# Sums of squares of the q/k norm: four float32 products a tile in place of twelve bfloat16 ones

## The chip, the cores and the metric

The program runs on one core of a Trainium2 chip. Its time is the device time of one execution in microseconds (us), from the first to the last instruction with what the launch adds around it. The core has five engines that run their own instruction streams: TensorE (PE; its weight loads are listed apart as PEld), VectorE (DVE), ScalarE (ACT), GpSimd (POOL) and SyncE (SP), which only issues transfers here. They wait for one another by semaphores.

## The reference

The reference is two layers of a decoder on 512 positions of width 2048, in float32. Each layer normalizes its input, projects it to queries, keys, values and a gate, attends, multiplies by the gate and projects back:

```python
q = rope(rms_norm(q.reshape(B, T, N_HEADS, HEAD_DIM), q_g), pos)      # 16 heads of 128
k = rope(rms_norm(k.reshape(B, T, N_KV_HEADS, HEAD_DIM), k_g), pos)   # 4 heads of 128
...
def rms_norm(x, g):
    y = xf * lax.rsqrt(jnp.mean(xf * xf, axis=-1, keepdims=True) + EPS)
    return (y * g.astype(jnp.float32)).astype(x.dtype)
```

The first layer picks the 128 best keys of each query by an indexer before it attends; the second attends within blocks of 256, which is the whole causal past for these 512 positions. What matters here is the mean of `xf * xf` over the 128 elements of a head, for each of 16 query heads and 4 key heads of a layer, and each of the 512 positions.

## The kernel before, in words

**Tiles and quarters.** Every projection is worked off in tiles of 128 output columns, held transposed: 128 features on the partitions, 512 positions along the row. A weight is cut into a high and a low part (`whi`, `wlo`), an input into `xh` and `xl`, and a product is made of three: high by high, high by low, low by high (lines 222 to 224). A tile has 16 blocks of the inner dimension, so 48 products of 128x512, and it is issued in four *quarters* of twelve products. The list `units` holds all quarters in their order; the main loop takes one unit a turn, and its index is the time `now` of the program text. In a layer come the values, then for each of four groups a k tile, four q tiles and the gate tiles of these heads, and then 16 output tiles `z_o`.

**What sets the order.** TensorE and SyncE execute in the order in which the text emits instructions, throughout. ScalarE, VectorE and GpSimd do so in the opening (46 units); behind it a scheduler orders their instructions ahead of the run. `later(k, f)` puts a step `f` behind the products of the unit `k` turns on. Two lists of steps concern the norm. A k tile: `s1` (1 turn after its last quarter), `s2` (2), `s2b` (4), `s3` (5), `s4` (6), `s5` (7), `s6` (8). A q tile: `s1` (1), `s2` (2), `s2b` (4), `s3` (5).

**The norm.** The features lie on the partitions, so a sum over a head's 128 features is a sum over partitions, and TensorE makes it: the squares are the stationary operand, a column of ones moves through, and the 128 sums of a block of positions come out as one column. `s1` builds a `Norm`: ScalarE squares the tile (line 306) and rounds the square to bfloat16 (316). `middle`, in `s2`, subtracts the rounded part on VectorE, rounds the rest (320) and subtracts again, so that three bfloat16 parts `b0`, `b1`, `b2` hold the float32 square. `sums`, in `s2b`, multiplies four blocks of positions by three parts, twelve products of one column, into a bank of PSUM (`cs_q` or `cs_k`, line 327). In `s3` VectorE adds the layer's own term (`u_q`, `u_k`) and GpSimd takes the power -1/2 (`sc`, `rk`). For a k tile, `bcast` in `s4` then spreads `rk` over the partitions (`b_k`, line 257), and `s5` and `s6` multiply and cut the key tile. The banks of `cs`, `b_k` and a layer's statistics are one and the same (`psm`, one buffer).

**The statistics of a layer.** `layer_stats` sums the squares of the layer's input over the width. It uses `colsum` (lines 246 to 251), which multiplies the float32 sum of squares `ssum` by a float32 column of ones, in four products (`ss`, line 250), once a layer.

**Paced extra work.** The selection in the first layer is a list `fill` of VectorE steps; the main loop takes from it as long as the paced count of VectorE's work (`dve.until`) lies behind the turn. While the list is not empty, the low parts of weights are cut on GpSimd. When it is empty, the mask opens the first layer's heads (`A.open`), which then attend at distances of 7 or 8 turns.

Of the kernel before, what the change touches and what calls it, by code (L numbers as in the profile page):

```python
# [26 lines left out]
BF = mybir.dt.bfloat16  # L27
AF = mybir.ActivationFunctionType
OP = mybir.AluOpType
# [3 lines left out]
P = 128  # L33
# [3 lines left out]
NQ = T // P  # L37
# [68 lines left out]
def build(tc, a):  # L106
    nc = tc.nc
# [14 lines left out]
    def t512(tag, name, dt=F32, bufs=None, p=None, cols=T):  # L122
        return (p or kp).tile([P, cols], dt, tag=tag, name=name, **({"bufs": bufs} if bufs else {}))
# [4 lines left out]
    def small(tag, name, bufs=2):  # L128
        return kp.tile([P, NQ], F32, tag=tag, name=name, bufs=bufs)

    def ps(tag, name, bufs):
        return pp.tile([P, T], F32, tag=tag, name=name, bufs=bufs)

    pss = lambda name: ps("s", name, 3)
    psm = lambda name: ps("sm", name, 1)
# [10 lines left out]
    def later(k, f, first=False):  # L146
        fs = hooks.setdefault(now[0] + k, [])
        fs.insert(0 if first else len(fs), f)
# [6 lines left out]
    dve, gps = Paced(nc.vector, 1.05e-3), Paced(nc.gpsimd, 2.1e-3)  # L155
# [72 lines left out]
    def add(t, quarters=None):  # L228
        units.extend((t, q) for q in quarters or range(KT // t.kts))
# [7 lines left out]
    ones_bf = cp.tile([P, 1], BF, name="ones_bf")  # L237
# [8 lines left out]
    def colsum(sq, name):  # L246

        t = psm(name)
        for j in range(NQ):
            nc.tensor.matmul(t[:, j:j + 1], lhsT=sq[:, j * P:(j + 1) * P], rhs=ones, start=True, stop=True)  # L250
        return t[:, :NQ]

    def bcast(col, name):

        t = psm(name)
        for j in range(NQ):
            nc.tensor.transpose(t[:, j * P:(j + 1) * P], col[:, j:j + 1].to_broadcast([P, P]), ident)
        return t

    def cut_hi(hi, src):  # L260
        nc.scalar.copy(hi, src)

    def cut_lo(lo, src, hi):
        dve.tensor_tensor(lo, src, hi.bitcast(F32), op=OP.subtract)
# [28 lines left out]
    def rope(z, g, name):  # L293

        t1 = tmp(f"t1_{name}")
        t2 = tmp(f"t2_{name}")
        dve.scalar_tensor_tensor(t1, z, g, cos, op0=OP.mult, op1=OP.mult)
        for o, i in ((0, 64), (64, 0)):
            dve.scalar_tensor_tensor(t2[o:o + 64], z[i:i + 64], g[i:i + 64], sin[i:i + 64],
                                           op0=OP.mult, op1=OP.mult)  # L300
        dve.tensor_tensor(t1, t1, t2, op=OP.add)
        return t1

    def square(z, name):
        sq = t512("sq", f"sq_{name}", bufs=1)
        nc.scalar.activation(sq, z, AF.Square)
        return sq

    class Norm:


        def __init__(self, z, name):
            self.name = name
            self.sq = square(z, name)
            self.b = [t512(f"b{i}", f"b{i}_{name}", BF, bufs=1) for i in range(3)]
            nc.scalar.copy(self.b[0], self.sq)

        def middle(self):
            dve.tensor_tensor(self.sq, self.sq, self.b[0], op=OP.subtract)
            nc.scalar.copy(self.b[1], self.sq)  # L320
            dve.tensor_tensor(self.b[2], self.sq, self.b[1], op=OP.subtract)

        def sums(self):
            t = psm(f"cs_{self.name}")
            for j in range(NQ):
                for i in range(3):
                    nc.tensor.matmul(t[:, j:j + 1], lhsT=self.b[i][:, j * P:(j + 1) * P], rhs=ones_bf,
                                     start=i == 0, stop=i == 2)
            return t[:, :NQ]

    def k_tile(Y, g):
        n = f"k{Y.L}_{g}"
        early = Y.L == 0 and g == 1
        v = SimpleNamespace()

        def s1():
            v.n = Norm(v.z, n)
            v.r = rope(v.z, Y.kg, n)

        def s2():  # L340
            v.n.middle()

        def s2b():
            v.s = v.n.sums()

        def s3():
            u = small("u", f"u_{n}")
            dve.scalar_tensor_tensor(u, v.s, 1.0 / P, Y.ce, op0=OP.mult, op1=OP.add)
            v.rk = small("rk", f"rk_{n}", 1)
            gps.tensor_tensor(v.rk, u, mhalf, op=OP.pow)  # L350

        def s4():
            v.b = bcast(v.rk, f"b_{n}")

        def s5():
            dve.tensor_tensor(v.r, v.r, v.b, op=OP.mult)
            p, th, tl = (bp, "bh15", "bl15") if early else (kp, "kh", "kl")
            kh = t512(th, f"kh_{n}", F32R, p=p)
            kl = t512(tl, f"kl_{n}", F32R, p=p)
            cut_hi(kh, v.r)  # L360
            Y.K[g] = (kh, kl)

        def s6():
            cut_lo(Y.K[g][1], v.r, Y.K[g][0])

        def done(z):
            v.z = z
            for k, f in ((1, s1), (2, s2), (4, s2b), (5, s3), (6, s4), (7, s5), (8, s6)):
                later(k, f)
        add(Tile(n, Y.w[16 + g], Y.X, done))  # L370

    def v_tiles(Y):
# [12 lines left out]
    def q_tile(Y, h):  # L385
        n = f"q{Y.L}_{h}"
        early = Y.L == 0 and h < 8
        v = SimpleNamespace()

        def s1():  # L390
            v.n = Norm(v.z, n)
            v.r = rope(v.z, Y.qg, n)

        def s2b():
            v.s = v.n.sums()

        def s2():
            v.n.middle()
            p, th, tl = (bp, f"bh{9 - h % 4}", f"bl{9 - h % 4}") if early else (kp, "qh", "ql")
            qh = t512(th, f"qh_{n}", F32R, p=p)  # L400
            ql = t512(tl, f"ql_{n}", F32R, p=p)
            cut_hi(qh, v.r)
            cut_lo(ql, v.r, qh)
            Y.q[h] = (qh, ql)

        def s3():
            u = small("u", f"u_{n}")
            dve.tensor_tensor(u, v.s, Y.cq, op=OP.add)
            sc = small("sc", f"sc_{n}", 6)
            gps.tensor_tensor(sc, u, mhalf, op=OP.pow)  # L410
            Y.sc[h] = sc

        def done(z):
            v.z = z
            Y.qslot[h] = now[0]
            for k, f in ((1, s1), (2, s2), (4, s2b), (5, s3)):
                later(k, f)
        add(Tile(n, Y.w[h], Y.X, done))

    def g_tile(Y, h):  # L420
# [132 lines left out]
    def mixer_tiles(Y):  # L553
        if Y.L:
            v_tiles(Y)
        for g in range(HEADS // GROUP):
            k_tile(Y, g)
            for h in range(GROUP * g, GROUP * g + GROUP):
                q_tile(Y, h)
                if h == 1 and not Y.L:  # L560
                    v_tiles(Y)
                if h % GROUP:
                    g_tile(Y, h - 1)
            g_tile(Y, h)
# [29 lines left out]
    def x_square(kt):  # L594
        if kt == 0:
            nc.scalar.activation(ssum, xs[kt], AF.Square)
        else:
            sq = square(xs[kt], f"x{kt}")
            gps.tensor_tensor(ssum, ssum, sq, op=OP.add)
# [159 lines left out]
    def evac0(n, z):  # L759
        def s1():  # L760
            r = res.pop((0, n))
            dve.tensor_tensor(r, z, r, op=OP.add)
            nc.sync.dma_start(h1[n], r)
            take(X1, n, r, gains[:, KT + n:KT + n + 1], 1)
            if n == 0:
                ssum1.append(t512("S", "ssum1", cols=1280)[:, :T])
                nc.scalar.activation(ssum1[0], r, AF.Square)
            else:
                sq = square(r, f"h{n}")
                gps.tensor_tensor(ssum1[0], ssum1[0], sq, op=OP.add)  # L770
        later(1, s1)
        if n == KT - 1:
            later(4, lambda: layer_stats(B, ssum1[0]))
# [25 lines left out]
    for L, start, src in ((0, first_out, a["xT"]), (1, second_out, h1)):  # L799
        for i in range(start, start + 4 * KT):  # L800
            t, q = units[i]
# [121 lines left out]
```

## Time and profile before

| | |
|---|---|
| median of 3 runs | 1481.86 us (1481.7 to 1481.94) |
| the profiled execution's own time | 1481.96 us |
| its span, first to last instruction | 1480.0 us |
| busy: PE / DVE / ACT / POOL | 1472.1 / 912.7 / 698.7 / 149.1 us |

All rows below come from one profiled execution. A row of the timeline begins with the start and the duration in us. Products overlap in TensorE, so durations add up to more than the time they take: the distance between two starts is what a product costs the stream. A group's row gives the busy time, the mean of one in ns, and the idle time of its engine ahead of it with what ended it.

### The profile page before, as it was taken

Reading aid. Unit: us, or ns where it says so; the run is one execution under the profiler, and the core shown is the slowest. Engines: PE = TensorE matmul, PEld = TensorE weight load, DVE = VectorE, ACT = ScalarE, POOL = GpSimd, SP = SyncE. Lnnn points to the kernel's source line nnn. Section 1 sums busy time; section 2 is a strip of 40 time slices with the busy share of each in tenths; the row PEclk is TensorE's granted clock in tenths of the full one; section 3 lists DMA queues with packets and bytes.
Section 4 is the critical chain, followed back from the end, with each engine's and each line's share of the span. In section 5 each row is a group of like instructions: output and inputs, shape, how many; then the busy total and the mean of one; then the engine's idle time right before and its main releaser. Section 6 shows DMA issues by size and latency. Waiting matters only on the chain.

```text
span 1480.0 us, 20172 instructions
## 1 busy us (share of the span) xinstructions
PE 1472.1 (99%) x7318; PEld 1233.0 (83%) x7318; DVE 912.7 (62%) x1845; ACT 698.7 (47%) x1332; POOL 149.1 (10%) x123
## 2 busy tenths in 40 slices
PE   9999999999999999999999999999999999999998
PEld 6998888888888888888888888888888888888887
DVE  6998976767567666643333376676676576643232
ACT  6874244555446445533332345554555455442221
POOL 0442420000010010111110010000000000000000
PEclk9999999999999999999999999999999999999999
DMA  7332324535433524444443224334434433454442
GB/s 252 108 99 74 100 97 145 153 111 144 134 111 118 156 90 139 143 156 150 149 143 114 100 90 152 107 122 144 134 110 123 151 122 107 143 164 150 142 143 92
DMA packets 77283, 191.78 MB, mean 130 GB/s; under 512 B 8704, under 2 KB 25856, under 8 KB 77184
## 3 DMA queue, kind: packets, MB, share of 16 engines
q1 hardware_dynamic: 76896, 189.98, 41.2%
q8 instruction: 57, 0.93, 0.3%
q10 hardware_dynamic: 288, 0.52, 0.1%
q14 instruction: 42, 0.34, 0.1%
HBM read 161.11 MB, written 29.36 MB: 129 GB/s over the span
## 4 chain that ended last, share of the span: by engine, by line
PE 97%; DMA 1%; DVE 1%; ACT 1%; issue 0%; SPq 0%; DVEq 0%; POOL 0%; ACTq 0%; POOLq 0%
PE z_q L222 8%; PE z_g L222 8%; PE z_g L224 8%; PE z_q L224 8%; PE z_g L223 8%; PE z_q L223 8%; PE z_o L223 8%; PE z_o L222 8%; PE z_o L224 8%; PE o L527 4%; PE z_k L222 2%; PE z_v L205 2%; PE z_k L224 2%; PE z_k L223 2%; PE z_v L207 2%; PE z_v L206 2%
## 5 line engine op out<-in xcount | busy, mean ns | idle before, releaser
L222 PE MATMUL z_q<-xh,whi_q 128*128 128x512 f32 x512 | 202.9, 396 | 0.0
L222 PE MATMUL z_g<-xh,whi_g 128*128 128x512 f32 x512 | 202.1, 395 | 0.0
L224 PE MATMUL z_g<-xh,wlo_g 128*128 128x512 f32 x512 | 200.1, 391 | 0.0
L224 PE MATMUL z_q<-xh,wlo_q 128*128 128x512 f32 x512 | 199.9, 390 | 0.0
L223 PE MATMUL z_g<-xl,whi_g 128*128 128x512 f32 x512 | 199.4, 390 | 0.0
L222 PE MATMUL z_o<-bh,whi_o 128*128 128x512 f32 x512 | 199.4, 389 | 0.0
L223 PE MATMUL z_q<-xl,whi_q 128*128 128x512 f32 x512 | 199.4, 389 | 0.0
L224 PE MATMUL z_o<-bh,wlo_o 128*128 128x512 f32 x512 | 199.2, 389 | 0.0
L223 PE MATMUL z_o<-bl,whi_o 128*128 128x512 f32 x512 | 199.2, 389 | 0.0
L89 DVE TENSOR_TENSOR wlo_o<-raw_o,whi_o 128x512 fp32r<-128x512 f32 x128 | 88.8, 693 | 163.4 <-ACT whi_o L192 163.4
L192 ACT CAST whi_o<-raw_o 128x512 fp32r<-128x512 f32 x128 | 79.7, 623 | 229.4 <-PE z_o L223 216.8
L192 ACT CAST whi_g<-raw_g 128x512 fp32r<-128x512 f32 x128 | 79.3, 620 | 166.3 <-PE z_q L223 120.9
L89 DVE TENSOR_TENSOR wlo_g<-raw_g,whi_g 128x512 fp32r<-128x512 f32 x123 | 84.5, 687 | 107.6 <-ACT whi_g L192 107.3
L192 ACT CAST whi_q<-raw_q 128x512 fp32r<-128x512 f32 x128 | 79.1, 618 | 103.9 <-PE z_q L223 43.4
L224 PEld LDWEIGHTS z_q<-xh,wlo_q 128*128 128x128 f32 x512 | 96.1, 188 | 20.9
L224 PEld LDWEIGHTS z_g<-xh,wlo_g 128*128 128x128 f32 x512 | 96.1, 188 | 20.8
L222 PEld LDWEIGHTS z_o<-bh,whi_o 128*128 128x128 f32 x512 | 96.1, 188 | 20.0
L224 PEld LDWEIGHTS z_o<-bh,wlo_o 128*128 128x128 f32 x512 | 96.1, 188 | 19.9
L223 PEld LDWEIGHTS z_o<-bl,whi_o 128*128 128x128 f32 x512 | 96.1, 188 | 19.8
L223 PEld LDWEIGHTS z_q<-xl,whi_q 128*128 128x128 f32 x512 | 96.2, 188 | 18.9
L223 PEld LDWEIGHTS z_g<-xl,whi_g 128*128 128x128 f32 x512 | 96.2, 188 | 18.6
L222 PEld LDWEIGHTS z_q<-xh,whi_q 128*128 128x128 f32 x512 | 96.1, 188 | 18.6
(164 smaller groups left out, 2687.0 us busy)
## 6 DMA issues: line engine op xcount, KB each, us to landing
d<-u SPq DMA_DIRECT2D x64, 320.0 KB, 3.8
pt<-d SPq DMA_DIRECT2D x128, 160.0 KB, 3.6
raw_q<-w_a SPq DMA_DIRECT2D x32, 512.0 KB, 4.1
raw_g<-w_a SPq DMA_DIRECT2D x32, 512.0 KB, 3.9
raw_q<-w_b SPq DMA_DIRECT2D x32, 512.0 KB, 4.4
raw_g<-w_b SPq DMA_DIRECT2D x32, 512.0 KB, 4.3
raw_o<-w_ao SPq DMA_DIRECT2D x26, 512.0 KB, 3.6
raw_o<-w_bo SPq DMA_DIRECT2D x26, 512.0 KB, 3.6
```

The costliest lines, as they stand in the source:

```text
L89: return f(out, *args, **kw)
L192: nc.scalar.copy(hi, r)
L205: nc.tensor.matmul(z, lhsT=xh, rhs=hi, start=first, stop=False)
L206: nc.tensor.matmul(z, lhsT=xh, rhs=lo, start=False, stop=False)
L207: nc.tensor.matmul(z, lhsT=xl, rhs=hi, start=False, stop=last)
L222: nc.tensor.matmul(o, lhsT=hi[:, k], rhs=xh, start=kt == 0, stop=False)
L223: nc.tensor.matmul(o, lhsT=hi[:, k], rhs=xl, start=False, stop=False)
L224: nc.tensor.matmul(o, lhsT=lo[:, k], rhs=xh, start=False, stop=kt == KT - 1)
L527: nc.tensor.matmul(o[:, q], lhsT=Y.V[kt][l][:, f], rhs=r[:, t], start=m == 0 and c == 0, stop=m == 4 and c == 2)
```

## The change

The Norm keeps the float32 squares and gives them to `colsum`. The parts, their roundings and subtractions go, and `middle` with them. The squares have two buffers instead of one. With one step less in between, the sums and what follows them stand one turn earlier: 3, 4, 5, 6, 7 for a k tile and 3, 4 for a q tile.

```diff
     def square(z, name):
-        sq = t512("sq", f"sq_{name}", bufs=1)
+        sq = t512("sq", f"sq_{name}", bufs=2)
...
             self.sq = square(z, name)
-            self.b = [t512(f"b{i}", f"b{i}_{name}", BF, bufs=1) for i in range(3)]
-            nc.scalar.copy(self.b[0], self.sq)
-
-        def middle(self):
-            dve.tensor_tensor(self.sq, self.sq, self.b[0], op=OP.subtract)
-            nc.scalar.copy(self.b[1], self.sq)
-            dve.tensor_tensor(self.b[2], self.sq, self.b[1], op=OP.subtract)
 
         def sums(self):
-            t = psm(f"cs_{self.name}")
-            for j in range(NQ):
-                for i in range(3):
-                    nc.tensor.matmul(t[:, j:j + 1], lhsT=self.b[i][:, j * P:(j + 1) * P], rhs=ones_bf,
-                                     start=i == 0, stop=i == 2)
-            return t[:, :NQ]
+            return colsum(self.sq, f"cs_{self.name}")
...
-        def s2():
-            v.n.middle()
-
...
-            for k, f in ((1, s1), (2, s2), (4, s2b), (5, s3), (6, s4), (7, s5), (8, s6)):
+            for k, f in ((1, s1), (3, s2b), (4, s3), (5, s4), (6, s5), (7, s6)):
...
         def s2():
-            v.n.middle()
...
-            for k, f in ((1, s1), (2, s2), (4, s2b), (5, s3)):
+            for k, f in ((1, s1), (2, s2), (3, s2b), (4, s3)):
```

In TensorE's order, these rows stand at the sums of the second layer's first k tile before. `z_q_0` is the next q tile; the first three products of the block, each with its weight load, are shown, and the block goes on to its twelfth, behind which the q tile `z_q_1` begins.

```order
L223 MATMUL z_q_0_8048<-xl_15_7677,whi_q_0_3_8073 128x512
L224 MATMUL z_q_0_8048<-xh_15_7676,wlo_q_0_3_8074 128x512
L327 LDWEIGHTS b_k_0_8063
L327 MATMUL cs_k_0_8128<-ones_bf,b_k_0_8063 128x1
L327 LDWEIGHTS b_k_0_8064
L327 MATMUL cs_k_0_8128<-ones_bf,b_k_0_8064 128x1
L327 LDWEIGHTS b_k_0_8065
L327 MATMUL cs_k_0_8128<-ones_bf,b_k_0_8065 128x1
```

And these stand there now, in the same engine, around the same tile.

```order
L223 MATMUL z_q_0_7748<-xl_11_7054,whi_q_0_2_7744 128x512
L224 MATMUL z_q_0_7748<-xh_11_7053,wlo_q_0_2_7745 128x512
L250 MATMUL cs_k_0_7803<-ones,sq_k_0_7761 128x1 x4
L222 MATMUL z_q_0_7748<-xh_12_7133,whi_q_0_3_7769 128x512
L223 MATMUL z_q_0_7748<-xl_12_7134,whi_q_0_3_7769 128x512
```

The sums have moved from behind the last quarter of `z_q_0` to behind its third quarter, and four products of the float32 square (`x4`) take the place of twelve. Neither the products of the projections nor their order have changed there.

On GpSimd, these are the rows where the first layer's first k tile gets its scales, before: `rk_k_0` is the power of that tile, `rc` that of the layer's statistics, `acc` the scores of the indexer, and `wlo` a low part of a weight.

```order
L89 TENSOR_TENSOR rc_1369<-ms_1367,mhalf 128x4
L89 AFFINE_SELECT acc_119<-acc_119 128x128
L89 AFFINE_SELECT acc_118<-acc_118 128x128
L89 AFFINE_SELECT acc_117<-acc_117 128x128
L89 TENSOR_TENSOR rk_k_0_1565<-u_k_0_1563,mhalf 128x4
L89 TENSOR_TENSOR wlo_q_1_3_1580<-raw_q_1_2_1340,whi_q_1_3_1579 128x512
```

And now:

```order
L89 TENSOR_TENSOR rc_1369<-ms_1367,mhalf 128x4
L89 TENSOR_TENSOR rk_k_0_1504<-u_k_0_1502,mhalf 128x4
L89 AFFINE_SELECT acc_119<-acc_119 128x128
L89 AFFINE_SELECT acc_118<-acc_118 128x128
L89 AFFINE_SELECT acc_117<-acc_117 128x128
L89 TENSOR_TENSOR wlo_q_1_3_1566<-raw_q_1_2_1340,whi_q_1_3_1565 128x512
```

The power for the k tile has moved ahead of the three selects on the scores. The selection's list is emptied one turn earlier, and the first four heads of the first layer attend one turn earlier than before; the other 28 heads stand at the turns where they stood.

## Rows read from the trace of the kernel before

**Rows 1.** Page, part 1: busy us, share of the span, instructions of each engine.

```profile
PE 1472.1 (99%) x7318; PEld 1233.0 (83%) x7318; DVE 912.7 (62%) x1845; ACT 698.7 (47%) x1332; POOL 149.1 (10%) x123
```

**Rows 2.** Page, part 2: TensorE's granted clock in 40 slices, in tenths.

```profile
PEclk9999999999999999999999999999999999999999
```

**Rows 3.** Page, part 4: the chain that ended last, by engine.

```profile
PE 97%; DMA 1%; DVE 1%; ACT 1%; issue 0%; SPq 0%; DVEq 0%; POOL 0%; ACTq 0%; POOLq 0%
```

**Rows 4.** Windows: start:end, length, busy us (count) of PE, PEld, DVE, ACT, POOL, PEclk, DMA.

```profile
37.00:140.00 103.00, 101.27 (x549) 92.54 (x548) 94.31 (x139) 73.32 (x149) 38.71 (x30) 1.00 0.31 95
222.00:610.00 388.00, 388.00 (x2018) 325.54 (x2017) 265.19 (x575) 205.44 (x408) 23.68 (x17) 1.00 0.44 130
800.00:806.00 6.00, 6.00 (x32) 5.08 (x31) 1.71 (x5) 1.17 (x2) 1.02 (x1) 1.00 0.29 87
```

**Rows 5.** Waits of PE: who waited for whom, us in total, times, longest.

```profile
PE is L676 <- DVE Q L89: 1.3, 2, 1.0
...
PE b_k L257 <- POOL rk_k L89: 0.2, 1, 0.2
```

**Rows 6.** Groups of PE by form: busy us, mean ns | idle before.

```profile
L327 PE MATMUL cs_q<-ones_bf,b_q 128*128 128x1 bf16 x384 | 14.5, 164 | 0.0
...
L327 PE MATMUL cs_k<-ones_bf,b_k 128*128 128x1 bf16 x96 | 3.6, 164 | 0.0
L250 PE MATMUL ss<-ones,ssum 128*128 128x1 f32 x16 | 1.9, 239 | 0.0
```

**Rows 7.** Timeline of PE around a q tile: start us, duration us, instruction.

```profile
142.09 0.45 PE L327 MATMUL cs_q<-ones_bf,b_q 128*128 128x1 bf16 x12
142.41 0.48 PE L205 MATMUL z_v<-whi_v,xh 128*128 128x512 f32 x1
142.73 0.39 PE L206 MATMUL z_v<-wlo_v,xh 128*128 128x512 f32 x1
142.96 0.40 PE L207 MATMUL z_v<-whi_v,xl 128*128 128x512 f32 x1
```

**Rows 8.** Timeline of PE at the statistics of the second layer.

```profile
802.46 0.94 PE L250 MATMUL ss<-ones,ssum 128*128 128x1 f32 x8
803.26 0.49 PE L205 MATMUL z_v<-whi_v,xh 128*128 128x512 f32 x1
803.59 0.40 PE L206 MATMUL z_v<-wlo_v,xh 128*128 128x512 f32 x1
803.82 0.40 PE L207 MATMUL z_v<-whi_v,xl 128*128 128x512 f32 x1
```

**Rows 9.** Groups of PEld (weight loads) by form.

```profile
L327 PEld LDWEIGHTS <-b_q 128*128 128x128 bf16 x384 | 11.7, 96 | 8.4 <-issue 8.4
...
L250 PEld LDWEIGHTS ss<-ones,ssum 128*128 128x128 f32 x16 | 2.1, 191 | 0.2
```

**Rows 10.** Timeline of ACT: the square of the second layer's first k tile.

```profile
847.90 0.59 ACT L306 ACTIVATE sq_k<-z_k 128x512 f32<-128x512 f32 x1
```

**Rows 11.** Timeline of PE one quarter before that tile's sums, and at them.

```profile
855.56 0.39 PE L222 MATMUL z_q<-xh,whi_q 128*128 128x512 f32 x1
...
858.28 0.45 PE L327 MATMUL cs_k<-ones_bf,b_k 128*128 128x1 bf16 x12
```

**Rows 12.** Timeline of PE at the first k tile's spreading.

```profile
135.53 0.39 PE L224 MATMUL z_q<-xh,wlo_q 128*128 128x512 f32 x1
136.12 0.65 PE L257 MATMUL b_k<-ident,rk_k 128*128 128x128 f32 x4 [0.21 <-POOL rk_k L89]
```

**Rows 13.** Groups of DVE by form: the two subtractions of a q tile.

```profile
L89 DVE TENSOR_TENSOR sq_q<-sq_q,b_q 128x512 f32<-128x512 f32 x32 | 22.0, 687 | 0.6
...
L89 DVE TENSOR_TENSOR b_q<-sq_q,b_q 128x512 bf16<-128x512 f32 x32 | 21.7, 678 | 0.0
```

**Rows 14.** Groups of ACT by form: the two roundings of a q tile.

```profile
L316 ACT CAST b_q<-sq_q 128x512 bf16<-128x512 f32 x32 | 19.8, 620 | 1.0
...
L320 ACT CAST b_q<-sq_q 128x512 bf16<-128x512 f32 x32 | 19.8, 618 | 23.4 <-DVE sq_q L89 23.4
```

## The prediction

> **What bounds the kernel now.** I read the busy line first: TensorE's products are busy for 1472.1 of 1480.0 us, VectorE for 62% and ScalarE for 47% of the span [rows 1]. The next thing to look for is whether anything but TensorE stands in the chain that ended last: it is TensorE for 97% of it [rows 3], at a granted clock that reads 9 in every slice, which is full speed, 2.4 GHz [rows 2]. The windows then say where TensorE's 7.9 us of idle time lie: 388.00 of 388.00 us are busy where layer 0 attends, and 1.73 of 103.00 us are idle between 37 and 140 us [rows 4]. Of TensorE's waits, 1.3 us are for an index query's parts and 0.2 us for the first k tile's scales [rows 5]. So the end of this kernel is the length of TensorE's stream. What is taken off VectorE or ScalarE is worth at most what TensorE waits for them; what is added to or taken off the stream counts in full.
>
> **The change part by part.**
>
> Removed from the stream: 40 blocks of twelve bfloat16 products of one column each (32 q and 8 k tiles; 384 and 96 records, 164 ns each [rows 6]). Durations of single products overlap, so I take the cost from starts. A block begins at 142.09, the next product of the stream at 142.41, the one after that at 142.73, and the third at 142.96 [rows 7]. An undisturbed pitch is the last distance, 0.23. The block takes 0.32, and the product behind it 0.32 in place of 0.23, so a block costs 0.32 + 0.09 = 0.41 us. That is 0.027 us for each product with its weight load.
>
> Added to the stream: 40 calls of the column sum that the program already has for the statistics of a layer. It is the same line with the same forms: a float32 128x128 stationary operand, a float32 column of ones, four products, and products of 128x512 ahead of it and behind it. The trace before therefore shows the price. It holds 16 records of products [rows 6] and 16 of weight loads [rows 9] for two calls of four products: each float32 product runs as two passes, each with a weight load of its own. At 802.46 such a call begins, the next product starts at 803.26, the one after it at 803.59, then 803.82 [rows 8]. The call takes 0.80 us, and the product behind it 0.33 against 0.23, so 0.90 us. That is 0.10 us a pass, nearly four times the bfloat16 price, and eight passes instead of twelve do not make up for it. The weight loads show why: the mean one is 96 ns for a bfloat16 square part and 191 ns for the float32 sums [rows 9], and with one moving column there is little beside the load to take the time. The clock in the stretch around that call reads 1.00 [rows 4], so blocks of this sort do not by themselves lower it.
>
> The difference is 0.90 - 0.41 = 0.49 us a tile, and 40 x 0.49 = 19.6 us. A second reading agrees: the merged durations are 0.94 us for the call and 0.45 us for the twelve [rows 7, 8], again 0.49 apart.
>
> The Trainium skill, page "TensorE: Matmul & The Clock Gate", section "Weight-path perf modes — Fast Weight Load (FWL) and DoubleRow", says that a full load of 128 weights takes a faster path unless its type is FP32, and the section "LDWEIGHTS (loading the stationary operand)" gives columns / 1.2 ns, 107 ns for 128. It speaks against this change, and an estimate by it is 8 x 0.107 = 0.86 us for the call where the row shows 0.80, hence some 2.4 us more over 40 tiles; I keep the row.
>
> Removed from VectorE: two subtractions a tile, 687 and 678 ns over the 32 q tiles [rows 13], and the same two for 8 k tiles, so 40 x 1.37 = 55 us of its 912.7. Removed from ScalarE: two roundings a tile of 620 and 618 ns [rows 14], so 40 x 1.24 = 50 us of 698.7. Neither sets the end. As TensorE is idle in no part of 222 to 610 us [rows 4], these 105 us return nothing there; the ceiling for a return is the 7.9 us of idle time in the whole span, and most of that lies where no norm has begun or after the last product. I take 0 for it and keep the ceiling.
>
> Moved: the sums stand one quarter (twelve products) earlier. They wait for the square alone now. For the second layer's first k tile, the square ends at 847.90 + 0.59 = 848.49 [rows 10]; the sums stand at 858.28, and one quarter earlier is 855.56 [rows 11]. That leaves 7.1 us of cover, so the wait costs nothing. If the cover were gone, everything behind the sums in TensorE's strict order would wait with them. The k tile's addition, power and spreading keep their distances to the sums, since all move by the same quarter. In the first k tile, the spreading came at 136.12, 0.59 after the product before it, against 0.23 undisturbed [rows 12]: 0.36 us lost to a late power on GpSimd. That power now stands ahead of three selects in GpSimd's order, and I count this stall as gone: -0.3 us. The second buffer for squares removes a possible wait of ScalarE, which is not the bound. The first four heads of layer 0 attend one quarter earlier, because the paced list of selection steps is emptied sooner; that reorders four weight loads against the transfers of the turned weights, and adds no work. TensorE shows no wait for those transfers in layer 0's attending stretch [rows 4], so it is priced at 0.
>
> Sum: +19.6 - 0.3 = +19.3 us on the profiled execution's own 1481.96 us (span 1480.0 and 1.96 around it) gives 1501.3 us. That execution stands 0.10 us above the median of 1481.86.
>
> What the trace does not show is a float32 block that reads a square instead of the sum of squares. If its first load could not start under the product before it, each block would pay one load more, 0.19 us [rows 9]: +7.6 us, 1508.9. On the other side all 7.9 us of idle time might return: 1493.4. The rows nearest to both cases stand at the middle, so I take 1501.3, and a range of 1497.5 to 1505 that holds about half of the way to either end.
>
> **Rivals.**
>
> *The products are paid by count.* If a float32 product cost what a bfloat16 one costs, 0.027 us, a tile would pay 4 x 0.027 + 0.09 = 0.20 instead of 0.41, and 40 x 0.21 = 8.4 us would be gained: 1473.6, faster. For it speaks that one column is streamed in either case. Against it stand the two calls in the trace, which take 0.80 us each; the point of decision is a call of 0.32 us. Chance 0.03.
>
> *The lighter engines give time back.* VectorE and ScalarE lose 105 us of work; if TensorE's stalls went with it, up to 7.9 us return: 1493.4. Against it: nothing is idle in the attending stretches. Chance 0.05.
>
> *The earlier sums wait for the square.* Should ScalarE be late by a whole quarter (2.72 us from 855.56 to 858.28 [rows 11]) beyond its cover in, say, a quarter of the tiles, 10 x 2.72 = 27 us come on top: 1528.5. Against it: 7.1 us of cover, and a ScalarE with less to do. Chance 0.02.
>
> *Four passes a product.* Twice the passes of the row would be 1.60 + 0.10 = 1.70 us a call, 1.29 more than now, 40 x 1.29 = 51.6: 1533.3. The rows show two passes a product, so the trace speaks against it. Chance 0.01.
>
> The Trainium skill, page "FP8 and Floating Point Precision", section "TensorE Precision Notes", counts four passes for true FP32, and this last rival is that rule; the trace has eight records a call, not sixteen, and does not agree.
>
> **How the numbers follow.** The forecast, 1501.3 us, has 0.89, the rivals 0.03, 0.05, 0.02 and 0.01. The range leaves out what lies beyond half of the unknown costs, and the rivals except part of the second. About 0.2% (3 us) is what a measurement of this kernel can tell from no change. Every case but the first is slower by more than that: slower 0.96. The first rival gives faster 0.03, and a mixture of it with the forecast 0.01 for the same.
>
> **What would show it.** Right: 336 records of the column-sum line in place of 16, in 40 new blocks whose next product starts 0.80 us after their first; no new wait of TensorE in the list; idle time of TensorE about as before; VectorE some 55 us and ScalarE some 50 us lighter without any of it in the span; TensorE's clock unchanged. Wrong: blocks of 0.3 us (first rival), TensorE's waits for a square (third), idle time of TensorE that is down by several us (second), or a clock that falls around the blocks, which nothing here priced.

## The result, and the profile after

The changed kernel takes 1501.74 us (median of 4 runs, 1501.31 to 1501.85) against 1481.9 us before: a ratio of 1.0134, 95% interval 1.0123 to 1.0146. It is 19.8 us slower; 1501.3 had been forecast, in a range of 1497.5 to 1505.0.

The page of the changed kernel, the lines that answer to [rows 1 to 3]: span, busy us and share of each engine, granted clock, chain that ended last.

```profile
span 1499.8 us, 19706 instructions
...
PE 1492.7 (100%) x7158; PEld 1260.2 (84%) x7158; DVE 871.1 (58%) x1766; ACT 649.7 (43%) x1252; POOL 137.3 (9%) x122
...
PEclk9999999999999999999999999999999999999999
...
PE 96%; DVE 1%; DMA 1%; ACT 1%; issue 0%; DVEq 0%; SPq 0%; ACTq 0%
```

VectorE has lost 41.6 us of work and ScalarE 49.0, as against [rows 1], and the span is 19.8 us longer. TensorE is busy for 20.6 us more, the clock is as before, and the chain is still TensorE's.

The groups of PE and of PEld (weight loads) by form, which answer to [rows 6, 9]; busy us and mean ns.

```profile
L250 PE MATMUL cs_q<-ones,sq_q 128*128 128x1 f32 x256 | 30.3, 240 | 0.4 <-DVE t_k L89 0.4
...
L250 PE MATMUL cs_k<-ones,sq_k 128*128 128x1 f32 x64 | 7.7, 241 | 0.0
```

```profile
L250 PEld LDWEIGHTS cs_q<-ones,sq_q 128*128 128x128 f32 x256 | 33.4, 191 | 3.2 <-issue 0.8
```

With the 16 records of the layers' statistics the column-sum line now has 336: 40 blocks of eight passes, 240 ns a product and 191 ns a load, as the two calls in the trace before had it.

The timeline of PE at the sums of the second layer's first k tile, to be read against [rows 11] and, for the price, [rows 7, 8]: start, duration, instruction.

```profile
865.28 0.39 PE L224 MATMUL z_q<-xh,wlo_q 128*128 128x512 f32 x1
865.51 0.95 PE L250 MATMUL cs_k<-ones,sq_k 128*128 128x1 f32 x8
866.32 0.49 PE L222 MATMUL z_q<-xh,whi_q 128*128 128x512 f32 x1
866.64 0.40 PE L223 MATMUL z_q<-xl,whi_q 128*128 128x512 f32 x1
866.87 0.40 PE L224 MATMUL z_q<-xh,wlo_q 128*128 128x512 f32 x1
```

The block begins at 865.51, the next product at 866.32, the one after at 866.64, and the pitch is 0.23 again behind it: 0.81 + 0.32 - 0.23 = 0.90 us. The blocks of both layers show the same two distances, 0.80 to 0.81 and 0.32 to 0.33, except for three that stand behind a wait or behind the attention's short products (0.86 to 0.88). The timeline of the weight loads shows the difference, at a block behind a wait and at the block above:

```profile
139.85 0.97 PEld L250 LDWEIGHTS cs_q<-ones,sq_q 128*128 128x128 f32 x8 [0.77 <-issue]
...
865.28 1.08 PEld L250 LDWEIGHTS cs_k<-ones,sq_k 128*128 128x128 f32 x8
```

Above, the loading begins 0.23 us ahead of the block's first product, while the product before it runs; behind the wait it begins 0.03 us ahead of it (139.85 and 139.88). Twelve bfloat16 products cost 0.41 [rows 7], and 40 x 0.49 = 19.6 us.

The windows of the changed kernel, to answer [rows 4]: start:end, length, busy us (count) of PE, PEld, DVE, ACT, POOL, clock, DMA.

```profile
37.00:140.00 103.00, 101.10 (x543) 92.44 (x541) 93.04 (x137) 71.24 (x145) 38.83 (x30) 1.00 0.30 95
...
222.00:614.00 392.00, 392.00 (x1933) 332.96 (x1932) 245.48 (x538) 184.43 (x374) 18.01 (x17) 1.00 0.43 129
```

There is still no idle time in the stretch where layer 0 attends, and 1.90 us between 37 and 140, where there had been 1.73. In the whole span TensorE is idle for 7.1 us, against 7.9. The whole loss is work of TensorE.

Two waits have changed places. The timeline at the first k tile's spreading, which answers to [rows 12], and then at the first q tile's sums, which now wait:

```profile
133.19 0.39 PE L224 MATMUL z_q<-xh,wlo_q 128*128 128x512 f32 x1
133.41 0.60 PE L257 MATMUL b_k<-ident,rk_k 128*128 128x128 f32 x4
```

```profile
139.11 0.39 PE L224 MATMUL z_q<-xh,wlo_q 128*128 128x512 f32 x1
139.88 1.02 PE L250 MATMUL cs_q<-ones,sq_q 128*128 128x1 f32 x8 [0.38 <-DVE t_k L89]
140.76 0.48 PE L222 MATMUL z_q<-xh,whi_q 128*128 128x512 f32 x1
```

The spreading follows 0.22 us behind the product before it where it took 0.59: 0.36 us are won back. But the first q tile's sums start 0.77 us behind the product before them in place of 0.23. They wait for VectorE's `t_k`, the multiplication that reads the spread scales out of the one bank that `b_k` and `cs` share. That is 0.54 us lost, with 0.08 us more for a block whose first load is not hidden (0.88 in place of 0.80), and a wait that the prediction had not named. It stands in the list of TensorE's waits (who for whom, us in total, times, longest), where the row of `b_k` in [rows 5] is gone:

```profile
PE cs_q L250 <- DVE t_k L89: 0.4, 1, 0.4
```

The multiplication did not move along with the spreading, as the timeline of DVE shows, before and then after:

```profile
137.02 0.69 DVE L89 TENSOR_TENSOR t_k<-t_k,b_k 128x512 f32<-128x512 f32 x1
```

```profile
139.06 0.67 DVE L89 TENSOR_TENSOR t_k<-t_k,b_k 128x512 f32<-128x512 f32 x1
```

The spreading comes 2.71 us earlier than before (133.41 against 136.12), the multiplication 2.04 us later.

The square of the second layer's first k tile, from the timeline of ACT:

```profile
857.85 0.59 ACT L306 ACTIVATE sq_k<-z_k 128x512 f32<-128x512 f32 x1
```

It ends at 858.44, 7.07 us ahead of the sums at 865.51; 7.1 had been counted from [rows 10, 11].

### The profile page after: what moved, and what is told of

Its sections match the earlier page's. It is cut to its first block, busy times and chain, and to the rows that moved or that the text cites. A ratio compares the mean times of both kernels' runs of the same rounds, so it can differ in the third digit from the quotient of the medians.

```text
span 1499.8 us, 19706 instructions
## 1 busy us (share of the span) xinstructions
PE 1492.7 (100%) x7158; PEld 1260.2 (84%) x7158; DVE 871.1 (58%) x1766; ACT 649.7 (43%) x1252; POOL 137.3 (9%) x122
## 4 chain that ended last, share of the span: by engine, by line
PE 96%; DVE 1%; DMA 1%; ACT 1%; issue 0%; DVEq 0%; SPq 0%; ACTq 0%
PE z_g L222 8%; PE z_g L224 8%; PE z_g L223 8%; PE z_o L222 8%; PE z_o L224 8%; PE z_q L222 8%; PE z_o L223 8%; PE z_q L224 8%; PE z_q L223 8%; PE o L511 4%; PE z_k L222 2%; PE z_v L205 2%; PE z_k L224 2%; PE z_k L223 2%; PE z_v L207 2%; PE z_v L206 2%
## 5 line engine op out<-in xcount | busy, mean ns | idle before, releaser
L89 DVE TENSOR_TENSOR wlo_q<-raw_q,whi_q 128x512 fp32r<-128x512 f32 x123 | 84.1, 684 | 76.6 <-ACT whi_q L192 76.2
L223 PEld LDWEIGHTS z_o<-bl,whi_o 128*128 128x128 f32 x512 | 96.1, 188 | 19.8
```

What stands on the lines that cost most here:

```text
L89: return f(out, *args, **kw)
L223: nc.tensor.matmul(o, lhsT=hi[:, k], rhs=xl, start=False, stop=False)
```

## The experiments

The theory: a block of sums costs TensorE's stream its passes times a price that the type of the stationary operand sets, and nothing that happens on the other engines or by the earlier turns matters. The rivals: the turns (the sums now stand too early), relief (lighter engines give time back, so that the true price is higher), a fixed price for a block, and a price of the two-pass mode rather than of the load. Each is stated with its numbers ahead of the runs.

### The float32 sums at the turns of before

```diff
-            for k, f in ((1, s1), (3, s2b), (4, s3), (5, s4), (6, s5), (7, s6)):
+            for k, f in ((1, s1), (4, s2b), (5, s3), (6, s4), (7, s5), (8, s6)):
...
-            for k, f in ((1, s1), (2, s2), (3, s2b), (4, s3)):
+            for k, f in ((1, s1), (2, s2), (4, s2b), (5, s3)):
```

> The four float32 products are kept, but the sums and what follows them stand at the turns of the kernel before (4, 5, 6, 7, 8 and 4, 5). Theory of the stream (a block of float32 sums costs TensorE 0.90 us where twelve bfloat16 products cost 0.41, and nothing else matters): 1501.7 us, within 1 us of the changed kernel; the new 0.38 us wait of the first q tile's sums goes and the 0.2 us wait of the first k tile's spreading may come back. Rival, the turns (the sums stand too early and stall the stream, the products themselves cost about what they did): most of the 19.8 us goes, 1482 to 1487 us.

1500.9 us, ratio 1.0127 [1.0112, 1.0142], 19.0 us above the kernel before. Nearly the whole loss stays, so the turns are not its cause. The timeline of PE at the first q tile's sums in this kernel:

```profile
141.39 0.39 PE L224 MATMUL z_q<-xh,wlo_q 128*128 128x512 f32 x1
141.62 0.95 PE L250 MATMUL cs_q<-ones,sq_q 128*128 128x1 f32 x8
142.43 0.49 PE L205 MATMUL z_v<-whi_v,xh 128*128 128x512 f32 x1
```

They start 0.23 us behind the product before them: the wait for the shared bank is gone. The wait of the first k tile's spreading, which might have come back, did not:

```profile
135.47 0.39 PE L224 MATMUL z_q<-xh,wlo_q 128*128 128x512 f32 x1
135.69 0.60 PE L257 MATMUL b_k<-ident,rk_k 128*128 128x128 f32 x4
```

On GpSimd the power for this tile stands behind the three selects again (it starts at 134.50), but the block of sums ahead of the spreading is 0.49 us longer, and that covers the 0.36 us. The 0.8 us between this kernel and the changed one fit the one wait that is gone, 0.54 + 0.08 us, but the intervals overlap.

### Twelve bfloat16 products without the work that makes the parts

All twelve products read the first part, so the two lower parts are left out of the sums.

```diff
...
         def middle(self):
-            dve.tensor_tensor(self.sq, self.sq, self.b[0], op=OP.subtract)
-            nc.scalar.copy(self.b[1], self.sq)
-            dve.tensor_tensor(self.b[2], self.sq, self.b[1], op=OP.subtract)
+            pass
...
-                    nc.tensor.matmul(t[:, j:j + 1], lhsT=self.b[i][:, j * P:(j + 1) * P], rhs=ones_bf,
+                    nc.tensor.matmul(t[:, j:j + 1], lhsT=self.b[0][:, j * P:(j + 1) * P], rhs=ones_bf,
```

> The kernel before, without the two subtractions and the second rounding: the twelve bfloat16 products all read the first part, so the two lower parts of the squares are left out of the sums. VectorE and ScalarE are lighter by some 80 us, TensorE's stream is the same. Theory of the stream: 1481.6 us, at most 0.5 us below the kernel before. Rival, relief (lighter engines give time back to TensorE): below by up to its 7.9 us of idle time, 1474 us.

1481.75 us, ratio 0.9999 [0.9990, 1.0008]: no change. The busy line of its page:

```profile
PE 1472.4 (100%) x7318; PEld 1234.2 (83%) x7318; DVE 871.3 (59%) x1766; ACT 674.7 (46%) x1292; POOL 149.3 (10%) x122
```

VectorE is 41.4 us lighter and ScalarE 24.0 (65 us together, where some 80 had been expected), and TensorE is as busy as in [rows 1]. Relief returns nothing that this run can tell from zero; by its interval, 1.5 us at the most.

### The float32 sums with the parts made all the same

The changed kernel with the old `middle`, whose parts nothing reads, and one buffer of squares:

```diff
-        sq = t512("sq", f"sq_{name}", bufs=2)
+        sq = t512("sq", f"sq_{name}", bufs=1)
...
+            self.b = [t512(f"b{i}", f"b{i}_{name}", BF, bufs=1) for i in range(3)]
+            nc.scalar.copy(self.b[0], self.sq)
+
+        def middle(self):
+            rest = t512("rest", f"rest_{self.name}", bufs=1)
+            dve.tensor_tensor(rest, self.sq, self.b[0], op=OP.subtract)
+            nc.scalar.copy(self.b[1], rest)
+            dve.tensor_tensor(self.b[2], rest, self.b[1], op=OP.subtract)
...
```

> The changed kernel, with the three bfloat16 parts still made by ScalarE and VectorE though nothing reads them (the squares in one buffer). Theory of the stream: 1501.7 us within 1 us, as the changed kernel. Rival, relief: the changed kernel got something back from the lighter engines that is lost here, so slower than it by several us, up to 1509 us.

1502.11 us, ratio 1.0136 [1.0121, 1.0151], 0.4 us from the changed kernel. Its busy line:

```profile
PE 1492.2 (99%) x7158; PEld 1260.6 (84%) x7158; DVE 915.2 (61%) x1845; ACT 697.0 (46%) x1332; POOL 139.3 (9%) x123
```

VectorE and ScalarE are as loaded as before the change, TensorE is as busy as after it, and the time is that of after. With the run above this settles it from both sides: the time goes with TensorE's stream alone.

### Four, eight and twenty-four bfloat16 products

Three kernels change the count of two-byte passes in a block. Four: as the kernel without parts above, with one product per block of positions; it too leaves the two lower parts out. Eight: two parts, the second subtracted straight into bfloat16, one rounding and one subtraction a tile. Twenty-four: every block made twice.

```diff
# four
...
-                for i in range(3):
+                for i in range(1):
...
# eight
...
-            dve.tensor_tensor(self.sq, self.sq, self.b[0], op=OP.subtract)
-            nc.scalar.copy(self.b[1], self.sq)
-            dve.tensor_tensor(self.b[2], self.sq, self.b[1], op=OP.subtract)
+            dve.tensor_tensor(self.b[1], self.sq, self.b[0], op=OP.subtract)
...
-                for i in range(3):
+                for i in range(2):
...
# twenty-four
-            for j in range(NQ):
-                for i in range(3):
...
+            for c in range(2):
+                for j in range(NQ):
+                    for i in range(3):
...
```

> The kernel before without the two lower parts of the squares: four bfloat16 products a tile instead of twelve, no subtractions. Theory of the stream (0.027 us for each bfloat16 product with its load): 40 x 8 x 0.027 = 8.6 us less, 1473.0 us with the 0.3 us of the first k tile; this is also what four float32 products would have given if products were paid by count. Rival, a fixed price for each block (the switch between products of 512 columns and of one): 1481 us, hardly less.

> The kernel before with two bfloat16 parts of the squares instead of three: eight products, one rounding and one subtraction a tile. Theory of the stream (0.027 us a bfloat16 product with its load): 40 x 4 x 0.027 = 4.3 us less than the kernel before and some 0.3 us from the first k tile, 1477.4 us, below both kernels. Rival, a fixed price for each block: 1481 us or more.

> The kernel before with every block of sums made twice over (24 bfloat16 products a tile). Theory of the stream: 40 x 12 x 0.027 = 13 us more, 1494.8 us. Rival, a fixed price for each block: under 3 us more.

| products a block | us, median | ratio to before |
|---|---|---|
| 4 | 1473.64 | 0.9946 [0.9929, 0.9962] |
| 8 | 1477.92 | 0.9974 [0.9965, 0.9984] |
| 12 (before, beside them) | 1481.88 and 1481.59 | |
| 24 | 1493.7 | 1.0081 [1.0067, 1.0095] |

The timeline of PE at one q tile's block, in each of the three in this order:

```profile
298.01 0.25 PE L325 MATMUL cs_q<-ones_bf,b_q 128*128 128x1 bf16 x4
298.12 0.48 PE L222 MATMUL z_g<-xh,whi_g 128*128 128x512 f32 x1
298.45 0.39 PE L223 MATMUL z_g<-xl,whi_g 128*128 128x512 f32 x1
```

```profile
299.34 0.35 PE L325 MATMUL cs_q<-ones_bf,b_q 128*128 128x1 bf16 x8
299.56 0.48 PE L222 MATMUL z_g<-xh,whi_g 128*128 128x512 f32 x1
```

```profile
301.43 0.75 PE L328 MATMUL cs_q<-ones_bf,b_q 128*128 128x1 bf16 x24
302.05 0.48 PE L222 MATMUL z_g<-xh,whi_g 128*128 128x512 f32 x1
302.37 0.39 PE L223 MATMUL z_g<-xl,whi_g 128*128 128x512 f32 x1
```

From the start of the block to the next product: 0.11, 0.22 and 0.62 us, with 0.32 for twelve [rows 7]. That is (0.62 - 0.11) / 20 = 0.0255 us a pass and no fixed price worth naming; the 0.09 us that the product behind the block loses are there with four passes as with twenty-four. The 0.027 us of the expectations was the whole block over its twelve passes (0.32 / 12). The times follow: 40 x 12 x 0.0255 = 12.2 us more for twenty-four, measured 12.1. What the rival by count promised for four float32 products is there for four products of two bytes, at the price of the lower parts; the kernel with eight keeps two parts of three and still takes 3.7 us less than the kernel before.

### Every float32 block twice

```diff
-            return colsum(self.sq, f"cs_{self.name}")
+            t = psm(f"cs_{self.name}")
+            for c in range(2):
+                for j in range(NQ):
+                    nc.tensor.matmul(t[:, j:j + 1], lhsT=self.sq[:, j * P:(j + 1) * P], rhs=ones,
+                                     start=True, stop=True)
+            return t[:, :NQ]
```

> The changed kernel with every block of sums made twice over (eight float32 products, sixteen passes a tile). Theory of the stream with a price by pass (0.10 us): 40 x 8 x 0.10 = 32.2 us more than the changed kernel, 1533.9 us. Rival, a fixed price for each block (a switch into float32 sums that is paid once, the rest at the bfloat16 price of 0.027 us): 40 x 8 x 0.027 = 8.6 us more, 1510.3 us.

1538.22 us, ratio 1.038 [1.0364, 1.0396]: 36.5 us above the changed kernel, where 32.2 had been expected. A fixed price is out. The median lies between two pairs: two of the four runs took 1539.3 and 1539.54 us, the other two 1537.13 and 1537.05. The trace is that of the 1539.3. The timeline of PE at one of its blocks shows the first part of the miss:

```profile
307.22 1.84 PE L320 MATMUL cs_q<-ones,sq_q 128*128 128x1 f32 x16
308.93 0.49 PE L222 MATMUL z_q<-xh,whi_q 128*128 128x512 f32 x1
309.25 0.40 PE L223 MATMUL z_q<-xl,whi_q 128*128 128x512 f32 x1
```

The undisturbed blocks take 1.69 to 1.71 us where those of eight take 0.80 to 0.81, so the second eight passes cost some 0.89 and not 0.80: 0.111 us a pass. In a block of eight, the first load is hidden for some 0.08 us under the product before it, and a mean over eight had taken that for the price; the block of eight behind a wait, which hides next to none, took 0.88 = 8 x 0.11. 40 x 0.89 = 35.6 us, and the two shorter runs stand 35.4 above the changed kernel.

The second part is in the two longer runs. The windows of the traced one show it (start:end, length, PE busy with its count, clock, DMA share, GB/s), and so does the timeline of PE around the first q tile's block:

```profile
142.00:144.00 2.00, 2.00 (x11) 0.77 0.00 0
144.00:146.00 2.00, 2.00 (x7) 0.50 0.51 111
146.00:148.00 2.00, 2.00 (x9) 0.88 0.38 152
```

```profile
139.94 0.39 PE L224 MATMUL z_q<-xh,wlo_q 128*128 128x512 f32 x1
140.70 1.92 PE L320 MATMUL cs_q<-ones,sq_q 128*128 128x1 f32 x16 [0.38 <-DVE t_k L89]
142.48 0.48 PE L222 MATMUL z_q<-xh,whi_q 128*128 128x512 f32 x1
142.80 0.39 PE L223 MATMUL z_q<-xl,whi_q 128*128 128x512 f32 x1
...
144.24 0.63 PE L224 MATMUL z_q<-xh,wlo_q 128*128 128x512 f32 x1
144.67 0.63 PE L222 MATMUL z_q<-xh,whi_q 128*128 128x512 f32 x1
```

Here the block stands behind the wait for the shared bank. From 139.94, the last product ahead of it, to 142.48 no product of 512 columns starts; the granted clock then falls to 0.50, which is 1.2 GHz, and products that come every 0.23 us come every 0.43 (144.24 to 144.67) until it is back. Eight products at 0.2 us more are 1.6 us, and with 35.6 that makes 37.2; the profiled run stands 37.6 above the changed kernel. The windows from 0 to 139 and from 148 to 1530 us read 1.00, so there was no other fall. The mean clock reads 0.998 and 0.999 in the two longer runs and 1.000 in the two shorter ones, so the fall probably came in two of the four; only the first has a trace, and it is the times that speak, as 0.999 also stands beside a few runs of other kernels that are no longer than the rest. In the changed kernel, with the same wait and half the block, all four runs read 1.000.

### The doubled blocks at the turns of before

This kernel takes the wait ahead of that block away, and leaves the blocks; its edit is that of the first experiment on top of the one just shown.

> Eight float32 products a tile as in the doubled kernel, at the turns of the kernel before, where the first q tile's sums do not wait. In the doubled kernel the clock fell once, to 1.2 GHz, behind that wait and its block of sixteen passes. If wait and block together lowered it: no fall here, 40 x 0.89 = 35.6 us above the changed kernel at the old turns, 1536.5 us, and 1.6 us for the slow products and 0.5 us for the wait are gone from the doubled kernel. If a block of sixteen passes alone can lower it: falls in several of the 40 blocks, some 1.6 us each, well above 1538 us.

1536.51 us, ratio 1.037 [1.0354, 1.0385]. The line of its cores:

```profile
core 0: 1534.4 us, clock 1.000
```

The mean clock is 1.000 in all four runs, so sixteen passes alone did not lower it here, in 40 blocks a run. 1536.51 is 35.6 above the 1500.9 of the first experiment, which is the price by pass, and 0.6 below the two shorter runs of the doubled kernel, as much as the wait (0.54 + 0.08).

### One pass in the reduced float32 type

The squares are rounded to the reduced float32 type, which still has four bytes; the four products below leave four records, one pass each.

```diff
...
-            self.sq = square(z, name)
+            self.sq = square(z, name, F32R)
...
+            for j in range(NQ):
+                nc.tensor.matmul(t[:, 2 * j:2 * j + 2], lhsT=self.sq[:, j * P:(j + 1) * P], rhs=ones_r,
+                                 start=True, stop=True)
...
```

> The changed kernel with the squares rounded to the reduced float32 type by ScalarE, and four products of two columns of ones in that type: one pass a product, the lower bits of the squares are left out. If the price is that of a weight load of a 4-byte type (0.10 us a pass, whatever the mode): 4 x 0.10 + 0.10 = 0.50 us a tile, 0.09 more than the kernel before, 1485.5 us. If the two-pass mode alone is slow and a one-pass load goes at the bfloat16 price: 4 x 0.027 + 0.09 = 0.20 us, 1473.5 us. If a load of 0.19 us is not overlapped at all: 0.85 us a tile, 1499.5 us.

1483.62 us, ratio 1.0014 [1.0005, 1.0023]: near the first of the three, far from the others. The timeline of PE, and the group of its weight loads:

```profile
297.22 0.50 PE L321 MATMUL cs_q<-ones_r,sq_q 128*128 128x2 f32 x4
297.58 0.49 PE L222 MATMUL z_q<-xh,whi_q 128*128 128x512 f32 x1
297.91 0.40 PE L223 MATMUL z_q<-xl,whi_q 128*128 128x512 f32 x1
```

```profile
L321 PEld LDWEIGHTS cs_q<-ones_r,sq_q 128*128 128x128 f32 x128 | 19.1, 190 | 3.2 <-issue 0.8
```

Four passes take 0.36 us, which is 4 x 0.111 - 0.08. Half the passes cost half; so it is the pass with four-byte operands, not the two-pass mode, that has the price. That it is the load in that pass is argued and not shown: a load lasts 190 ns here, like the float32 one (191) and twice a bfloat16 one (96 [rows 9]), but in every run the moving column has the type of the squares. Nor does any run show whether the 0.0255 us of a two-byte pass are its load or the least distance of two products. The block costs 0.36 + 0.33 - 0.23 = 0.46 us against 0.41, 40 x 0.05 = 2.0 us, and 2.0 were measured; the 1485.5 expected had taken 0.10 a pass without the hidden part of the first.

### One float16 part

The runs point to few passes with two-byte operands. This version squares z/16 straight into float16 and takes the factor back behind the sums:

```diff
...
+            self.sq = t512("b0", f"b0_{name}", F16, bufs=1)
+            nc.scalar.activation(self.sq, z, AF.Square, scale=1.0 / 16)
...
+                    nc.tensor.matmul(t[:, j:j + 1], lhsT=self.sq[:, j * P:(j + 1) * P], rhs=ones_h,
+                                     start=True, stop=True)
...
-            dve.tensor_tensor(u, v.s, Y.cq, op=OP.add)
+            dve.scalar_tensor_tensor(u, v.s, 256.0, Y.cq, op0=OP.mult, op1=OP.add)
```

> The kernel before with one 16-bit part of the squares: ScalarE squares z/16 straight into float16, four float16 products a tile, no roundings and no subtractions, and the sums are scaled by 256 in the step behind them (the squares keep 11 bits). Theory of the stream (0.025 us a pass where the stationary operand has 2 bytes, as measured with 4, 8, 12 and 24 bfloat16 products): 0.21 us a tile instead of 0.41, 8 us less than the kernel before, 1473.7 us, the same as four bfloat16 products. Rival, by type (a float16 load goes at the 4-byte price of 0.11 us a pass): 0.46 us a tile, 1483.6 us.

1473.97 us, ratio 0.9949 [0.9937, 0.9962]: 0.5% faster than the kernel before and below the changed one too. Its timeline:

```profile
298.42 0.25 PE L325 MATMUL cs_q<-ones_h,b_q 128*128 128x1 f16 x4
298.54 0.48 PE L223 MATMUL z_g<-xh,whi_g 128*128 128x512 f32 x1
298.86 0.39 PE L224 MATMUL z_g<-xl,whi_g 128*128 128x512 f32 x1
```

A float16 block has the distances of the bfloat16 one, 0.12 and 0.32. The factor is there for the range of float16; inputs other than these were not run. Where 11 bits of each square are too few, the two bfloat16 parts above keep more, and they are still below both kernels.

## Why the prediction was right

- *The stream bounds the kernel.* Right: with 65 us off VectorE and ScalarE the time did not move, and with their work put back under the float32 sums it did not either.
- *The price of the blocks, 0.90 against 0.41 us.* Right: 0.90 in the trace after. The price was in the trace before, in two calls of a line that the change takes over, and the context (512 columns ahead and behind) was the same. The case that the range was kept open for, a first load that cannot start under the product before it, came in three blocks of the 40 and cost 0.06 to 0.08 us each, not the 0.19 of the prediction.
- *0.10 us a pass.* Good for a block of eight only. It was a mean that held the hidden 0.08 us of the first load; by the doubled blocks a pass costs 0.111. The term of the sum did not need it, the expectation of the doubled blocks did, and 3.4 us of its miss are due to it. The Trainium skill, page "TensorE: Matmul & The Clock Gate", section "LDWEIGHTS (loading the stationary operand)", gives columns / 1.2 ns, an estimate of 107 ns for 128 columns; the marginal 0.111 us agrees with that better than the 0.10 which I kept.
- *Relief of VectorE and ScalarE worth nothing.* Right in time. The 55 us for VectorE were too many: the busy time fell by 41.6. Records of neighbours overlap on VectorE (in the trace before, a subtraction of 0.68 us starts at 139.05 and the next instruction at 139.65), so a group's mean times its count is more than the busy time falls by. Besides, the groups that stayed add up to some 5 us more than before.
- *The earlier turns cost nothing.* Right for the square (7.07 us of cover). The wait that did come was another: the bank that the sums share with the k tile's spreading, 0.54 us once. The prediction followed the k tile's steps up to the spreading, but not to VectorE's multiplication, which has to read the bank before it is free, so that its sign of no new wait in TensorE's list did not hold. The wait ate what the first k tile's stall gave back (0.36), and the sum's last term, -0.3 us, should have been +0.2: 1481.96 + 19.6 + 0.2 = 1501.8. Nor were the earlier turns needed for the 0.36: at the old turns the longer block covers it.
- *How near it came.* The first product of the first k tile, ahead of any of these sums, starts between 101.5 and 102.5 us in the twelve traces. So the 0.4 us between forecast and result are no more than that, and an agreement to the tenth is luck.
- *The rivals.* By count: the block would have had to take less than 0.32 us; it takes 0.81. Four passes: eight records a block, not sixteen. The clock: unchanged here; with the block doubled behind the same wait it fell.

## What to carry to other kernels

For products of one column, count passes times the price of a pass in the operands' type, not products: here 0.0255 us a pass with two bytes and 0.111 with four, and a float32 product is two passes. By these prices, splitting into parts of two bytes pays on TensorE as long as there are fewer than some four such passes for one pass of four bytes; the work that makes the parts was free here, with VectorE busy for 62% of the span and ScalarE for 47%. Before a change, look whether the trace already holds the new form somewhere, and read its price from starts, the product behind it included.

## What the hardware showed that was not expected

- The mean of 0.10 us a pass for float32 sums is a first load partly hidden (some 0.08 us) and a marginal price of 0.111 us; the same float32 block takes 0.88 us behind a wait and 0.80 without one.
- Behind 2.54 us without a product of 512 columns, made of a wait and sixteen passes of one column, the clock fell once to 1.2 GHz and cost 1.6 us, in the traced run and probably in one more of four. The same sixteen passes without the wait, 40 times, left the mean clock at 1.000.
- The product behind a block loses 0.09 to 0.10 us whatever the block holds: four, eight, twelve, sixteen or twenty-four passes, two bytes or four.
